# HGRN2's values and K turned by VectorE and small transfers instead of TensorE, from the third unit on

## The chip, the core and the metric

The kernel runs on one core of a Trainium2 chip. A core has TensorE (PE, matrix products; the loading of its stationary operand is listed as PEld), VectorE (DVE), ScalarE (ACT), GpSimd (POOL) and SyncE (SP), whose queue issues nearly all transfers. Transfers run on 16 DMA engines. Everything lies in HBM at first; work is done on tiles of 128 partitions in SBUF, and TensorE writes to PSUM. The metric is the device time of one execution in microseconds, as the median of several runs. Before the change it is 2566.66 us (three runs, 2566.41 to 2567.90).

## The reference, cut to what matters

One decoder layer in float32, for 16 meta tokens and 256 prompt tokens, and for 8 further sequences with one new token each and a stored state. D_MODEL is 2048, D_FF 5504.

```python
x = layer_norm(ALPHA * x + 0.5 * swiglu(x, f1_g, f1_u, f1_d), ln1_g, ln1_b)
m, s_ret, s_hg = token_mixer(x, pos, s_ret, s_hg, prompt, w_in, lb, hg_norm_g, w_out)
x = layer_norm(ALPHA * x + m, ln2_g, ln2_b)
x = layer_norm(ALPHA * x + 0.5 * swiglu(x, f2_g, f2_u, f2_d), ln3_g, ln3_b)
```

The mixer projects x to ten parts of 2048 columns. Retention (8 heads of 256) uses q_r, k_r, v_r, g_r; HGRN2 (16 heads of 128) uses q_h, f_h, i_h, g_h; a_r and a_h gate the two branches. HGRN2 of one chunk is:

```python
f = lb + (1.0 - lb) * jax.nn.sigmoid(f_h)        # k = 1 - f, values v = i_h
o = jnp.einsum('bhij,bhjv->bhiv', A, v) + jnp.einsum('bhid,bhdv->bhiv', q * jnp.exp(b), S)
S_new = jnp.exp(b_last)[..., None] * S + jnp.einsum('bhjd,bhjv->bhdv', k_dec, v)
```

Outputs are the two groups of tokens and the new states of both branches for both groups.

## The kernel before

All 280 tokens (16 meta, 256 prompt, 8 sampled) stand as columns; features stand on partitions. A weight block is 128x128. Products keep float32 precision by splitting both operands into an upper and a lower part: three matmuls a block (`xh,whi`, `xl,whi`, `xh,wlo`, line L218). Weights come in units of 8 blocks, 512 KB each: SP loads `raw` (L185), ScalarE casts it to `whi` (L188), VectorE takes the difference `wlo` (L189). `raw`, `whi` and `wlo` have three buffers each, so a load waits until VectorE has used up the unit three before, and a cast until TensorE has.

The stages are: first FFN (up, down), mixer with its input projection (`pj_...`), output projection (`wo`), second FFN. The mixer goes over eight units u, each one head of retention and two of HGRN2. For a unit, `project` runs ten groups of two output tiles: f, q_h, i_h, q_r, k_r, v_r of unit u, and then four groups of gates (g_r with a_r, g_h with a_h, twice) of unit u-1's outputs. A group is 16 dense steps, one for each block of the inner dimension, with six matmuls a step; a group ends in `evacuate`.

TensorE's order is the order in which the program is written. After each dense step `pump` counts every thread down by one and lets those at zero issue their next piece. HGRN2's thread (`mix_hg`) is started when i_h is evacuated, retention's (`mix_ret`) when v_r is. A `yield n` in a thread is a pause of n dense steps. So the numbers behind `yield` and in `start` say between which dense matmuls a piece of the mixer stands. The order on the other engines and on SP's queue is set by a scheduler from data dependences and priorities; weight loads have high priority. Eight completion semaphores go round over SP's transfers, so a transfer waits for the one eight places before it.

In HGRN2's thread the steps that matter here are: the values v (features on partitions) are transposed to `vt` with tokens on partitions (tile `vth`; L875, copied out at L879), together with the short `ends` of meta and sampled tokens (L878); after the levels of decay products, `turned(h)` transposes K of each head (L982, copied to `kth` at L983); `load` and `values` fetch the sampled states (`smh`) and broadcast values (`vbh`), each behind a one-column copy on GpSimd (L769, L773) that makes them wait; `samples` updates the sampled states; `pst` (L1022, L1024) multiplies K and v to the states, which VectorE scales and adds (`Sh`, L1027) and SP stores (`out_sgp`, L1030); `pq` (L1039) and `po` (L1050, L1051) make the outputs. Retention's thread transposes its own v and k (L1107, L1114), makes `psr` (L1168), loads two megabytes of sampled states (`smr`, L1095), scales them on ScalarE (L1192), adds to them on VectorE (L1198) and stores them (`out_srs`, L1202), then makes `pqr` (L1211) and `por` (L1226).

## Time and profile before

| what | before |
|---|---|
| median of the runs | 2566.66 us |
| span of the profiled execution | 2563.9 us |
| instructions | 56275 |
| PE busy | 2553.4 us |
| DVE busy | 1702.8 us |
| ACT busy | 1392.2 us |
| bytes moved | 536.26 MB, 209 GB/s in the mean |
| granted TensorE clock | 1.000 |

The table's span is that of one profiled execution; the page gives no other time for it, and the runs' median is 2.8 us above its span. A view by lines groups instructions by line, engine and tiles: a line such as `L875 PE MATMUL pt<-ident,v` reads "line 875, TensorE, writes pt from ident and v". Durations of matmuls in it overlap, since matmuls are pipelined: the time from one start to the next is what TensorE's order costs. In a view of waits a line is "engine and tile <- what it waited for: us in total, times, longest". In a timeline a row is start, duration, engine, line, operation, tiles, shape, count, and in brackets the idle time before it. A unit of the mixer from the third on takes the same 126.3 us each (the first f of the fourth unit starts at 1085.64, of the fifth at 1211.98).

### The profile page before, as it was taken

Reading aid. Unit: us, or ns where it says so; the run is one execution under the profiler, and the core shown is the slowest. Engines: PE = TensorE matmul, PEld = TensorE weight load, DVE = VectorE, ACT = ScalarE, POOL = GpSimd, SP = SyncE. Lnnn points to the kernel's source line nnn. Section 1 sums busy time; section 2 is a strip of 40 time slices with the busy share of each in tenths; the row PEclk is TensorE's granted clock in tenths of the full one; section 3 lists DMA queues with packets and bytes.
Section 4 is the critical chain, followed back from the end, with each engine's and each line's share of the span. In section 5 each row is a group of like instructions: output and inputs, shape, how many; then the busy total and the mean of one; then the engine's idle time right before and its main releaser. Section 6 shows DMA issues by size and latency. Waiting matters only on the chain.

```text
span 2563.9 us, 56275 instructions
## 1 busy us (share of the span) xinstructions
PE 2553.4 (100%) x23424; PEld 2534.4 (99%) x23424; DVE 1702.8 (66%) x2827; ACT 1392.2 (54%) x2186; POOL 57.0 (2%) x152
## 2 busy tenths in 40 slices
PE   9999999999999999999999999999999999999999
PEld 9999999999999999999999999999999999999998
DVE  6444544475569878777777777777885555556555
ACT  5444444444456767767676666675564444444443
POOL 0000000000000000000000000000000000000000
PEclk9999999999999999999999999999999999999999
DMA  7555555555555876767676767675556565565554
GB/s 244 183 187 183 187 182 184 186 182 186 184 201 180 287 265 232 264 214 260 212 264 215 259 223 255 224 239 188 196 190 197 194 197 195 194 196 195 195 195 149
DMA packets 156897, 536.26 MB, mean 209 GB/s; under 512 B 17952, under 2 KB 25952, under 8 KB 156640
## 3 DMA queue, kind: packets, MB, share of 16 engines
q1 hardware_dynamic: 156352, 532.37, 62.0%
q8 instruction: 183, 3.00, 0.5%
q14 instruction: 74, 0.61, 0.1%
q10 hardware_dynamic: 288, 0.29, 0.0%
HBM read 501.99 MB, written 30.61 MB: 208 GB/s over the span
## 4 chain that ended last, share of the span: by engine, by line
PE 96%; DVE 2%; ACT 0%; issue 0%; DMA 0%; SPq 0%; ACTq 0%; DVEq 0%
PE up L218 36%; PE dn L218 19%; PE pj_i_h L218 3%; PE pj_g_r L218 3%; PE pj_q_h L218 3%; PE pj_g_h L218 3%; PE pj_a_r L218 3%; PE pj_a_h L218 3%; PE pj_f L218 3%; PE pj_q_r L218 3%; PE pj_k_r L218 3%; PE wo L218 3%; PE pj_v_r L218 3%; DVE wlo L189 1%; PE pqr L1211 1%; PE psr L1168 0%
## 5 line engine op out<-in xcount | busy, mean ns | idle before, releaser
L189 DVE TENSOR_TENSOR wlo<-raw,whi 128x1024 fp32r<-128x1024 f32 (+1 forms) x869 | 1062.2, 1223 | 740.7 <-ACT whi L188 737.3
L188 ACT CAST whi<-raw 128x1024 fp32r<-128x1024 f32 (+1 forms) x870 | 905.7, 1042 | 909.2 <-PE up L218 411.0
L218 PE MATMUL up<-xh,whi 128*128 128x280 f32 (+1 forms) x2624 | 725.6, 280 | 0.6 <-ACT whi L188 0.6
L218 PE MATMUL up<-xh,wlo 128*128 128x280 f32 (+1 forms) x2624 | 725.8, 280 | 0.4 <-DVE wlo L189 0.3
L218 PE MATMUL up<-xl,whi 128*128 128x280 f32 (+1 forms) x2624 | 725.4, 279 | 0.0
L218 PEld LDWEIGHTS up<-xh,wlo 128*128 128x128 f32 x2624 | 492.6, 189 | 1.0 <-DVE wlo L189 1.0
L218 PEld LDWEIGHTS up<-xh,whi 128*128 128x128 f32 x2624 | 492.6, 189 | 0.8 <-ACT whi L188 0.8
L218 PEld LDWEIGHTS up<-xl,whi 128*128 128x128 f32 x2624 | 492.6, 189 | 0.0
L218 PE MATMUL dn<-hh,whi 128*128 128x280 f32 (+1 forms) x1376 | 384.7, 280 | 0.0
L218 PE MATMUL dn<-hh,wlo 128*128 128x280 f32 (+1 forms) x1376 | 384.3, 279 | 0.0
L218 PE MATMUL dn<-hl,whi 128*128 128x280 f32 (+1 forms) x1376 | 384.3, 279 | 0.0
L218 PEld LDWEIGHTS dn<-hh,whi 128*128 128x128 f32 x1376 | 260.1, 189 | 0.1
L218 PEld LDWEIGHTS dn<-hl,whi 128*128 128x128 f32 x1376 | 260.1, 189 | 0.1
L218 PEld LDWEIGHTS dn<-hh,wlo 128*128 128x128 f32 x1376 | 260.1, 189 | 0.0
L218 PE MATMUL pj_k_r<-xh,whi 128*128 128x280 f32 x256 | 74.2, 290 | 0.0
L218 PE MATMUL pj_g_r<-xh,whi 128*128 128x264 f32 x256 | 74.0, 289 | 0.0
L218 PE MATMUL pj_v_r<-xh,whi 128*128 128x280 f32 x256 | 73.8, 288 | 0.0
L218 PE MATMUL pj_v_r<-xh,wlo 128*128 128x280 f32 x256 | 72.4, 283 | 0.3 <-DVE wlo L189 0.3
L218 PE MATMUL pj_g_h<-xh,whi 128*128 128x264 f32 x256 | 72.7, 284 | 0.0
L218 PE MATMUL pj_k_r<-xh,wlo 128*128 128x280 f32 x256 | 72.4, 283 | 0.0
L218 PE MATMUL pj_v_r<-xl,whi 128*128 128x280 f32 x256 | 72.3, 283 | 0.0
L218 PE MATMUL pj_k_r<-xl,whi 128*128 128x280 f32 x256 | 72.3, 283 | 0.0
(421 smaller groups left out, 5263.4 us busy)
## 6 DMA issues: line engine op xcount, KB each, us to landing
raw<-in_w_up SPq DMA_DIRECT2D x343, 512.0 KB, 4.1
raw<-in_w_in SPq DMA_DIRECT2D x320, 512.0 KB, 4.3
raw<-in_w_dn SPq DMA_DIRECT2D x172, 512.0 KB, 3.5
smr<-in_sr SPq DMA_DIRECT2D x32, 512.0 KB, 5.0
out_srs<-smr SPq DMA_DIRECT2D x32, 512.0 KB, 6.7
raw<-in_w_out SPq DMA_DIRECT2D x32, 512.0 KB, 3.9
vbr<-vrd SPq DMA_DIRECT2D x32, 256.0 KB, 4.1
smh<-in_sg SPq DMA_DIRECT2D x16, 512.0 KB, 5.2
```

Source lines behind the costliest of these rows:

```text
L188: nc.scalar.copy(hi[:, j:jn, :], raw[:, j:jn, :])
L189: nc.vector.tensor_tensor(out=lo[:, j0:j1, :], in0=raw[:, j0:j1, :], in1=hi[:, j0:j1, :].bitcast(F32), op=ALU.subtract)
L218: nc.tensor.matmul(o, w, t, start=start, stop=stop)
L1211: nc.tensor.matmul(pq[32 * j : 32 * j + 32, :256], qdr_at[c][:, 32 * b : 32 * b + 32], sms[2 * e + c][:, j, :], start=e + c == 0, stop=e + ...
```

## The change

From the third unit on (u > 1, or c0 > 2), v and K are no longer transposed by TensorE. VectorE turns 32x32 blocks within a tile, and 16 transfers of 32 partitions x 4 x 32 elements put the blocks in their places, one after two dense steps each, issued by a small thread of their own (`turned_over`).

- For v, VectorE reads the projection's PSUM directly (two instructions of 128x256) into the tile `v`, the transfers go to `vt`, and ScalarE copies the 16 first and 16 last columns of each head to `ends`. The two copies of v by ScalarE, the two by GpSimd, four transposes and two copies out of PSUM fall away.
- For K, VectorE turns both heads in one instruction (128x512) into the tile of k, which is dead by then, and the transfers go to the tile of f, also dead. Four transposes and two copies out of PSUM fall away. The waits of `load(1)` and `values(1)` now look at these tiles.
- The pause ahead of `pst` becomes 30 for 5, the one behind it 20 for 45.
- Retention's thread is started with 5 for 3 in these units, and a later pause in it is 13 for 15.

```diff
                 elif n == "i_h":
-                    v = st.pop("i_h", None)
-                    if v is None:
+                    v, vt = st.pop("i_h", None), tmp("vth", TURNED)
+                    ends = tmp("ends", (P, 2, 2, NMETA))
+                    if c0 > 2:
+                        z = squared(tmp("v", (P, 2, T)))
+                        for j, o in enumerate((o0, o1)):
+                            nc.vector.transpose(z[:, j].rearrange("p b t -> p (b t)"), o[:, NMETA:LP])
+                            nc.scalar.copy(ends[:, j, 0, :], o[:, :NMETA])
+                            nc.scalar.copy(ends[:, j, 1, :], o[:, T - NMETA : T])
+                        turned_over(vt, z, 2)
+                    elif v is None:
                         v = tmp("v", (P, 2, T))
                         nc.scalar.copy(v[:, 0, :], o0)
                         nc.scalar.copy(v[:, 1, :], o1)
-
-                    start(mix_hg(c0 // 2, st["f"], st["k"], st["q"], v), {0: 20, 2: 46}.get(c0, 4))
+                    start(mix_hg(c0 // 2, st["f"], st["k"], st["q"], v, ends, vt), {0: 20, 2: 46}.get(c0, 4))
...
-                    start(mix_ret(c0 // 2, st["q_r"], st["k_r"], v), 24 if c0 == 2 else 3)
+                    start(mix_ret(c0 // 2, st["q_r"], st["k_r"], v), {0: 3, 2: 24}.get(c0, 5))
...
+            TURNED = (P, 2, 2, P)
+            squared = lambda x: x.rearrange("p h t -> p (h t)")[:, : 4 * P].rearrange("p (h b t) -> p h b t", h=2, b=2)
...
+            def turned_over(out, z, pause):
+
+                def transfers():
+                    for i in range(0, P, 32):
+                        for j in range(0, P, 32):
+                            nc.sync.dma_start(out[j : j + 32, :, :, i : i + 32], z[i : i + 32, :, :, j : j + 32])
+                            yield pause
+
+                start(transfers(), 1)
...
-            def mix_hg(u, f, k, q, v):
+            def mix_hg(u, f, k, q, v, ends, vt):
...
-                ends = tmp("ends", (P, 2, 2, NMETA))
-                nc.gpsimd.tensor_copy(ends[:, :, 0, :], v[:, :, :NMETA])
-                nc.gpsimd.tensor_copy(ends[:, :, 1, :], v[:, :, T - NMETA :])
+                if u < 2:
+                    nc.gpsimd.tensor_copy(ends[:, :, 0, :], v[:, :, :NMETA])
+                    nc.gpsimd.tensor_copy(ends[:, :, 1, :], v[:, :, T - NMETA :])
...
-                    nc.gpsimd.tensor_copy(sms[h][:, 0, :1], kts[0][:, 0, :1] if h else acc[:, 15:16])
+                    nc.gpsimd.tensor_copy(sms[h][:, 0, :1], (kts[0] if u < 2 else k)[:, 0, :1] if h else acc[:, 15:16])
...
-                    nc.gpsimd.tensor_copy(vbs[h][:, 0, :1], kts[1][:, 0, :1] if h else acc[:, 2 * P + 15 : 2 * P + 16])
+                    n = 32 if h and u > 1 else P
+                    nc.gpsimd.tensor_copy(vbs[h][:n, 0, :1], kts[1][:n, 0, :1] if h else acc[:, 2 * P + 15 : 2 * P + 16])
...
-                    pt = mx_bank("pt")
-                    for b in range(2):
-                        nc.tensor.transpose(pt[:, b * P : (b + 1) * P], v[:, h, NMETA + b * P : NMETA + (b + 1) * P], ident)
+                    if u < 2 or h:
+                        pt = mx_bank("pt")
+                    if u < 2:
+                        for b in range(2):
+                            nc.tensor.transpose(pt[:, b * P : (b + 1) * P], v[:, h, NMETA + b * P : NMETA + (b + 1) * P], ident)
...
-                kts = []
+                kts = [squared(f)[:, h] for h in range(2)] if u > 1 else []
 
                 def turned(h):
+                    if u > 1:
+                        if h == 0:
+                            z = squared(k)
+                            nc.vector.transpose(z.rearrange("p h b t -> p h (b t)"), K[:, :, NMETA:])
+                            turned_over(squared(f), z, 2)
+                        return
...
-                    yield 4 if u == 0 else 5
+                    yield 4 if u == 0 else 30
...
-                yield (8, 11, 45)[min(u, 2)]
+                yield (8, 11, 20)[min(u, 2)]
...
-                yield (11 if u == 0 else 15) + 2 * calm
+                yield (11, 15, 13)[min(u, 2)] + 2 * calm
```

How this moves instructions shows in three places, all in the fourth unit (u=3). The first is TensorE around K's first pair of transposes (`ptk`) before the change, between two dense steps of k_r (the numbers behind the names are those of buffers):

```order
L218 MATMUL pj_k_r_14433<-xl_9_9272,whi_14546 128x280
L218 MATMUL pj_k_r_14433<-xh_9_9271,wlo_14547 128x280
L982 MATMUL ptk<-ident,K 128x128 x2
L218 MATMUL pj_k_r_14432<-xh_10_9275,whi_14546 128x280
L218 MATMUL pj_k_r_14432<-xl_10_9276,whi_14546 128x280
```

In the changed kernel k_r's dense steps follow each other there, while `pst`, which stood in v_r, now stands within the first g_h group, between its seventh and eighth step:

```order
L218 MATMUL pj_a_h_15043<-xh_6_9259,wlo_15121 128x264
L1050 MATMUL pst<-vm,km 128x128
L1052 MATMUL pst<-vth,f 128x128 x2
L1050 MATMUL pst<-vm,km 128x128
L1052 MATMUL pst<-vth,f 128x128 x2
L218 MATMUL pj_g_h_15042<-xh_7_9263,whi_15120 128x264
```

The second place is SP's queue between k_r and the start of retention's transfers, in the changed kernel (`f<-k` are K's small transfers):

```order
L185 DMA raw_15044<-in_w_in 128x1024
L1030 DMA out_sgs<-smh 128x1024
L185 DMA raw_15119<-in_w_in 128x1024
L741 DMA f<-k 32x4x32 x2
L185 DMA raw_15167<-in_w_in 128x1024
L741 DMA f<-k 32x4x32 x5
L185 DMA raw_15209<-in_w_in 128x1024
L741 DMA f<-k 32x4x32
L749 DMA vrd<-vt_8636 8x256
L185 DMA raw_15251<-in_w_in 128x1024
L1184 DMA vbr<-vrd 128x512 x2
```

Before, only weight loads, `out_sgs` and `out_sgp` stood there; the small transfers of v stand likewise, in runs of 4, 3, 3 and 6, between the weight loads during q_r, and `out_sgp` now follows the second `out_srs`.

The third place is VectorE in the g_h group and behind it, where retention's sampled states (`smr`) are updated between the weights' differences (`wlo`). Before:

```order
L189 TENSOR_TENSOR wlo_15175<-raw_15173,whi_15174 128x8x128
L189 TENSOR_TENSOR wlo_15217<-raw_15215,whi_15216 128x8x128
L1198 SCALAR_TENSOR_TENSOR smr<-vbr,sro,smr 128x256 x5
L189 TENSOR_TENSOR wlo_15247<-raw_15245,whi_15246 128x8x128
L1198 SCALAR_TENSOR_TENSOR smr<-vbr,sro,smr 128x256 x3
L240 TENSOR_TENSOR gt<-gs,pj_g_h_15035 128x264
L189 TENSOR_TENSOR wlo_15277<-raw_15275,whi_15276 128x8x128
```

And in the changed kernel, the same four units of weights (`wlo_15211`, `wlo_15253`, `wlo_15283`, `wlo_15313`):

```order
L189 TENSOR_TENSOR wlo_15211<-raw_15209,whi_15210 128x8x128
L1226 SCALAR_TENSOR_TENSOR smr<-vbr,k_r,smr 128x256 x2
L1055 SCALAR_TENSOR_TENSOR Sh<-Sh,T_14522,pst 128x128 x4
L189 TENSOR_TENSOR wlo_15253<-raw_15251,whi_15252 128x8x128
L1226 SCALAR_TENSOR_TENSOR smr<-vbr,sro,smr 128x256 x2
L189 TENSOR_TENSOR wlo_15283<-raw_15281,whi_15282 128x8x128
L1226 SCALAR_TENSOR_TENSOR smr<-vbr,sro,smr 128x256 x5
L189 TENSOR_TENSOR wlo_15313<-raw_15311,whi_15312 128x8x128
```

`Sh` has come in ahead of the second of these, and the five updates that stood ahead of the third now stand ahead of the fourth.

6 lines of the change are left out of this document (3 added, 3 removed).

## The prediction

> **What bounds the kernel now.** I read the page first: the span, the busy times and the chain of waits.
>
> ```profile
> span 2563.9 us, 56275 instructions
> PE 2553.4 (100%) x23424; PEld 2534.4 (99%) x23424; DVE 1702.8 (66%) x2827; ACT 1392.2 (54%) x2186; POOL 57.0 (2%) x152
> PE 96%; DVE 2%; ACT 0%; issue 0%; DMA 0%; SPq 0%; ACTq 0%; DVEq 0%
> ```
>
> TensorE is busy all the time and is 96% of the chain. So the time is the sum of what TensorE issues, as long as nothing makes it wait. Next I cut one steady unit of the mixer, the fourth (u=3), into three stretches with the view of busy time by window; the columns are the stretch, its length, busy time and instructions of PE, PEld, DVE, ACT and POOL, the granted clock, the DMA share and GB/s.
>
> ```profile
> 1085.64:1168.00 82.36, 82.36 (x848) 81.84 (x847) 66.39 (x135) 56.60 (x111) 4.75 (x11) 1.00 0.64 216
> 1168.00:1194.00 26.00, 26.00 (x275) 24.96 (x274) 21.21 (x39) 15.90 (x24) 1.40 (x3) 1.00 0.84 281
> 1194.00:1211.98 17.98, 17.98 (x159) 17.88 (x158) 10.87 (x22) 12.30 (x25) 0.00 (x0) 1.00 0.77 275
> ```
>
> A unit takes 126.34 us, at full clock, with no gap on TensorE. But the slack beneath differs. ScalarE's casts of the weights (`whi`) tell it, by what they wait for. These are ScalarE's waits in two stretches of the same unit, 1120 to 1165 and then 1168 to 1194:
>
> ```profile
> ACT whi L188 <- PE pj_q_r L218: 4.6, 2, 2.9
> ...
> ACT whi L188 <- DMA raw<-in_w_in: 5.7, 3, 2.3
> ```
>
> In the first the cast waits for TensorE to give a buffer back, so the weights are early. In the second it waits for the transfer itself. How close that comes to TensorE, two rows of the timeline show: the last step of one 512 KB of weights (`wlo`, VectorE), and the first matmul that reads it (matched by counting the weights' units back from the end of the program).
>
> ```profile
> 1184.59 1.22 DVE L189 TENSOR_TENSOR wlo<-raw,whi 128x1024 fp32r<-128x1024 f32 x1
> 1186.05 0.28 PE L218 MATMUL pj_g_r<-xh,wlo 128*128 128x264 f32 x1
> ```
>
> The weights are ready at 1185.81 and needed at 1186.05: 0.24 us ahead. I call this the dip. It lies where retention loads and stores its sampled states, and recurs in every unit.
>
> **The change, part by part.** *Removed on TensorE.* Four pairs of transposes a unit, two of v (one of them with the `ends` transpose, which stays) and two of K. Their price on TensorE's path is not their recorded duration but by how much the matmuls behind them start later:
>
> ```profile
> 1121.97 0.28 PE L218 MATMUL pj_q_r<-xh,wlo 128*128 128x264 f32 x1
> 1122.09 0.38 PE L875 MATMUL pt<-ident,v 128*128 128x128 f32 x2
> 1122.22 0.36 PE L218 MATMUL pj_q_r<-xh,whi 128*128 128x264 f32 x1
> 1122.42 0.28 PE L218 MATMUL pj_q_r<-xl,whi 128*128 128x264 f32 x1
> 1122.53 0.28 PE L218 MATMUL pj_q_r<-xh,wlo 128*128 128x264 f32 x1
> ...
> 1140.10 0.28 PE L218 MATMUL pj_k_r<-xh,wlo 128*128 128x280 f32 x1
> 1140.22 0.38 PE L982 MATMUL ptk<-ident,K 128*128 128x128 f32 x2
> ...
> 1140.56 0.28 PE L218 MATMUL pj_k_r<-xl,whi 128*128 128x280 f32 x1
> 1140.68 0.28 PE L218 MATMUL pj_k_r<-xh,wlo 128*128 128x280 f32 x1
> ```
>
> Dense matmuls start 0.11 us apart (1122.42, 1122.53; 0.12 with 280 columns: 1140.56, 1140.68). From 1121.97 to the second matmul behind the first pair, at 1122.42, is 0.45; two steps would be 0.225, so the pair costs 0.22. K's pair: 1140.10 to 1140.56, 0.46 less 0.24, again 0.22. Each transpose thus costs what a dense matmul does, with no further price for breaking in, so I take the pair that leaves `ends` behind at 0.22 too. A unit saves 4 x 0.22 = 0.88 us, and the counts say that a unit has four of each transpose:
>
> ```profile
> L982 PE MATMUL ptk<-ident,K 128*128 128x128 f32 x32 | 6.1, 273 | 0.0
> L875 PE MATMUL pt<-ident,v 128*128 128x128 f32 x32 | 6.1, 273 | 0.0
> ```
>
> Of the eight units six change: 6 x 0.88 = **5.3 us**.
>
> *Added on VectorE.* Two turnings of 128x256 from PSUM and one of 128x512. The trace has none; the nearest rows are:
>
> ```profile
> 1135.24 0.43 DVE L677 SCALAR_TENSOR_TENSOR q_r<-pj_q_r,cos 128x264 f32<-128x264 f32 x1
> 1111.40 0.69 DVE L240 TENSOR_TENSOR Q<-q,f 128x512 f32<-128x512 f32 x1
> ```
>
> I take 2 x 0.43 + 0.69 = 1.55 us a unit, and twice that, 3.1, as the upper end; nothing can be under 0. They stand in the first stretch, where the weights wait for TensorE, and where VectorE is idle for 16 of 82 us: 0 on the path. Without that cover a unit would pay the 1.55 to 3.1. ScalarE loses two copies of v and four out of PSUM and gains four narrow ones: it gets lighter.
>
> *Added on SP and the DMA engines.* 32 transfers a unit, 16 KB each in 128-byte runs. One load of the kernel's start has exactly this size and number of packets (`lbt`), and one microsecond there held almost only small packets:
>
> ```profile
> lbt<-in_lb SPq DMA_DIRECT2D x1, 16.0 KB, 4.2
> 27.44 0.42 SPq L539 DMA_DIRECT2D lbt<-in_lb  x1
> ...
> DMA packets 228, 0.11 MB, mean 106 GB/s; under 512 B 212, under 2 KB 212, under 8 KB 227
> q1 hardware_dynamic: 227, 0.09, 32.7%
> q1 hardware_dynamic: 156352, 532.37, 62.0%
> ```
>
> SP is held 0.42 us by each. The longest run of them between two weight loads is six, 2.5 us, while the loads are a weight unit apart: 24 matmuls of 0.11 to 0.12, 2.7 to 2.9 us. So they fit, just. On the engines, 32.7% of 16 engines in that microsecond is 5.2 us for 227 packets, 23 ns each at most: 128 x 23 / 16 = 0.18 us a transfer, 5.9 us a unit. The upper end is the run's mean packet, nearly all of 4 KB: 62% x 16 x 2563.9 / 156352 = 163 ns, 1.3 us a transfer, 42 us a unit. The first stretch has 36% of 82 us free, 30 us. The first price disappears in it, the second does not (a rival). I take the first, from the row of the same size. The Trainium skill (DMA: Bandwidth & Descriptors, Specifications) says that writes under 512 B are read, modified and written; by that the price would lean to the upper end, but the small packets of this trace show no sign of it.
>
> *Moved.* HGRN2's state products (`pst`) leave `v_r` for the first `g_h` group, 25 steps later, and take their followers along: VectorE's `Sh`, ScalarE's copy, SP's two `out_sgp`. That is now inside the stretch of the dip. Retention starts two steps (12 matmuls, 1.35 us) later there, but its last part is where it was (13 for 15).
>
> ```profile
> 1154.95 0.28 PE L218 MATMUL pj_v_r<-xh,wlo 128*128 128x280 f32 x1
> ...
> 1156.31 0.28 PE L218 MATMUL pj_v_r<-xl,whi 128*128 128x280 f32 x1
> ...
> 1156.77 0.43 ACT L1025 COPY Sh<-pst 128x128 f32<-128x128 f32 x2
> 1157.93 1.12 DVE L1027 SCALAR_TENSOR_TENSOR Sh<-Sh,T,pst 128x128 f32<-128x128 f32 x4
> 1184.20 0.48 DVE L1198 SCALAR_TENSOR_TENSOR smr<-vbr,sro,smr 128x256 f32<-128x256 f32 x1
> ```
>
> `pst` costs TensorE 1.36 less 0.24, 1.12 us, in either place. In its new place it delays TensorE's need for the dip's weights by that 1.12, while VectorE gets 1.12 and ScalarE 0.43 more to do. Behind `Sh` on VectorE stands a `wlo`, and TensorE waits for that. On the other side, the dip's own `wlo` has two state updates ahead of it where it had five: 3 x 0.48 = 1.4 us less. I therefore put the dip at 0.24 + 1.12 + 1.4 - 1.12 - 0.43 = 1.2 us, no stall; the bounds are 2.7 us (ScalarE and VectorE hide theirs) and a stall (below). K's last transfer is issued some 45 steps less 31 before `pst`, 14 steps or 9 us, so 4.2 us of landing fit.
>
> **Sum.** 2563.9 - 5.3 = 2558.6 us of span. The median of the runs, 2566.66, is 2.8 above the profiled span; so 2566.66 - 5.3 = **2561.4 us**, 0.21% less. What a measurement tells from no change is 0.2%, 5.1 us, and the forecast lies almost on that line.
>
> **Rivals.** *The dip becomes a stall* (slower). Retention's work comes 1.35 later, `Sh` and the copy add 1.55, and only 0.24 of slack and the 1.12 of `pst` stand against it: 1.35 + 1.55 - 1.36 = 1.5 us a unit, 9.2 in all, 2570.6; if the 1.12 does not help, 2.7 a unit, 16, 2577. It outweighs the gain from 0.88 us a unit, and shows as slower from 0.88 + 0.86 = 1.7. For it: the weights there already wait for the DMA, at 84% share. Against it: the order of VectorE's rows, above. *A small stall*, 0.1 to 0.8 us a unit, takes the gain back: 2562 to 2566, no measurable difference. *The transfers cost like other packets* (slower): 42 us in 30 leaves 12 us late a unit, of which the two weight units in stock bridge at most 5.4; 6.6 x 6 - 5.3 gives about 2601. It decides from 30 us a unit, 117 ns a packet, five times the row's 23. *A transpose costs its recorded 273 ns*: 48 x 0.273 = 13.1 us, 2553.6. Against it stands the start of the next matmul, 0.13 us after that of the two. The Trainium skill (VectorE: DVE Perf Modes, The three transpose paths) gives 390 ns for a 128x128 on TensorE; by this the saving would be an estimated 18.7 us, which the trace's 0.11 contradicts. By the same page's Rules for kernel authors a 128x128 belongs on TensorE if PSUM will do as its destination: that speaks against this change, and at 0.11 each there is indeed little to win.
>
> **How the numbers follow.** The forecast has 0.68 (0.44 of it beyond 0.2%, 0.24 short of it, since the line is inside its own spread of some 0.7 us); the small stall 0.17; the stall that makes it slower 0.09; dear packets 0.03; dear transposes 0.03. Faster: 0.44 + 0.03 = 0.47. The same: 0.24 + 0.17 = 0.41. Slower: 0.09 + 0.03 = 0.12. The range runs from 2560.2 (a little more, where the dip in some runs already cost something) to 2566.5 (all of the gain lost to small stalls), and leaves out the three dear cases and the outermost of the forecast.
>
> **What would show it.** Right: TensorE's matmuls fewer by 48, a steady unit of 125.45 us instead of 126.34, PE still busy throughout 1168 to 1194, and the dip's `wlo` more than 1 us ahead of its matmul. Wrong: gaps of PE in front of a matmul that reads `wlo` or `whi` late in the `g_h` group or early in the second `g_r` group; ScalarE's casts waiting for DMA between `q_r` and `v_r`; a turning on VectorE over 1.4 us; or `pst` waiting for `f` or `vth`. The forecast fails if the six units are not each about 0.9 us shorter.

## The result, and the profile after

The changed kernel takes 2578.68 us (2577.52 to 2584.51) where the kernel before took 2566.6 us on the same chip. The ratio is 1.0052 with a 95% interval of 1.0037 to 1.0066: **slower by 0.5%**, where 2561.4 us had been forecast. The span of the profiled execution grew by 11.8 us. The 5.3 us that the removed transposes were to save must be added, so about 17 us of new stall have to be explained.

The page of the changed kernel, its span, its engines and its chain of waits:

```profile
span 2575.7 us, 56433 instructions
PE 2555.1 (99%) x23376; PEld 2532.6 (98%) x23376; DVE 1708.0 (66%) x2845; ACT 1382.1 (54%) x2174; POOL 45.9 (2%) x140
PE 87%; DVE 5%; DMA 4%; ACT 2%; issue 1%; SPq 0%; POOL 0%; ACTq 0%; DVEq 0%
```

TensorE has 48 matmuls fewer, as meant. But its share of the chain fell from 96% to 87%: VectorE, DMA and ScalarE, 2% together before, now hold 11% of the chain. The same unit as in the prediction (u=3) starts its f here, and the next unit here:

```profile
1089.42 0.28 PE L218 MATMUL pj_f<-xh,whi 128*128 128x280 f32 x1
...
1217.04 0.28 PE L218 MATMUL pj_f<-xh,whi 128*128 128x280 f32 x1
```

That is 127.62 us a unit, not the 125.45 expected; the next three take 127.75, 127.14 and 127.25. So each of these four has a stall of about 2 us. The third unit takes 136.46 where it took 133.39, and from the last unit's start to the first matmul of the output projection it is 172.67 us where it was 169.83: about 4 us of stall in each of these two, with the 0.88 saved. That is 15.6 of the 17 us; the rest lies outside, ahead of the third unit and in the output projection and behind it.

The busy times in the three stretches of this unit, at the same distances from its start as in the prediction (the last one is longer by what the unit grew):

```profile
1089.42:1171.78 82.36, 82.36 (x847) 81.84 (x846) 67.35 (x136) 56.40 (x110) 3.77 (x9) 1.00 0.70 218
1171.78:1197.78 26.00, 24.37 (x252) 23.52 (x254) 20.96 (x40) 14.51 (x22) 0.42 (x3) 1.00 0.83 276
1197.78:1217.04 19.26, 19.26 (x180) 18.58 (x172) 11.33 (x24) 12.12 (x24) 0.00 (x0) 1.00 0.86 291
```

The first stretch, which holds all the turning and all the small transfers, has no gap. TensorE stands in the second, the dip (24.37 of 26.00 us busy), although that stretch moves no more bytes than before (0.83 and 276 GB/s against 0.84 and 281). Rows of SP, VectorE and TensorE show in order how it comes about (times from the span's start; in brackets the idle time before):

```profile
1165.78 4.26 SPq L741 DMA_DIRECT2D f<-k  x5
...
1170.71 0.59 SPq L741 DMA_DIRECT2D f<-k  x1
1171.35 0.49 SPq L749 DMA_DIRECT2D vrd<-vt  x1
...
1173.92 0.85 SPq L1184 DMA_DIRECT2D vbr<-vrd  x2
...
1178.09 0.48 DVE L1226 SCALAR_TENSOR_TENSOR smr<-vbr,k_r,smr 128x256 f32<-128x256 f32 x1 [1.81 <-DMA vbr<-vrd]
...
1188.69 0.88 DVE L1226 SCALAR_TENSOR_TENSOR smr<-vbr,sro,smr 128x256 f32<-128x256 f32 x2 [2.64 <-DMA vbr<-vrd]
1189.48 1.22 DVE L189 TENSOR_TENSOR wlo<-raw,whi 128x1024 fp32r<-128x1024 f32 x1
1190.76 0.38 PE L218 MATMUL pj_g_r<-xh,wlo 128*128 128x264 f32 x1 [1.48 <-DVE wlo L189]
```

`vrd` and `vbr` bring retention's sampled values to all partitions. SP issues them behind K's last small transfers, and VectorE stands in front of its state updates until `vbr` has landed: 1.81 us for the first pair, 2.64 for the second. Behind the second wait in VectorE's order stands a `wlo`, and TensorE waits 1.48 us for it. In the kernel before, `vrd` and `vbr` were issued here:

```profile
1162.40 0.29 SPq L730 DMA_DIRECT2D vrd<-vt  x1
...
1164.42 0.80 SPq L1156 DMA_DIRECT2D vbr<-vrd  x2
```

Counted from the start of the unit that is 76.9 and 78.9 us before, 81.9 and 84.5 after: 5.0 and 5.6 us later, though retention's thread was moved by two steps, 1.35 us. (The unit before starts at 1085.48 by the row of its first f, not at 1085.64 as given above; its length is the same.) Moreover `v_r`, behind which retention starts, now ends 70.0 us into the unit instead of 72.0. By its place in the program `vrd` was thus due a little earlier than before, not later (one_straight, below, issues it at 75.6).

The chain of waits in the changed kernel says how one late wait is passed on (VectorE, then a weight load that can only start when VectorE gives its buffer back, then both halves of the split, then VectorE's own order):

```profile
1179.76 1.67 DVE smr L1226 x4
1181.43 1.15 DVE wlo L189
1182.59 5.39 DMA raw<-in_w_in
1188.08 1.04 ACT whi L188
1189.48 1.22 DVE wlo L189
1190.70 1.98 DVE smr L1226 x5
1192.68 1.15 DVE wlo L189
1193.87 0.38 PE pj_g_r L218
```

So the 1.48 us come mainly down this chain, from the first wait on `vbr`: the cast `whi` ended at 1189.12, and the second wait held the `wlo` back only from there to 1189.48.

One more loss follows in the profiled execution. Behind its longest wait for a `wlo` (1.86 us, in the last unit) the profile grants half the clock for 3.41 us; the columns are those of the busy times above:

```profile
1698.76:1702.19 3.43, 1.57 (x14) 1.38 (x13) 3.37 (x7) 1.59 (x3) 0.00 (x0) 1.00 0.76 307
1702.19:1705.60 3.41, 3.41 (x18) 3.41 (x18) 3.27 (x7) 0.35 (x2) 0.00 (x0) 0.50 0.90 279
```

Dense matmuls start 0.22 us apart there instead of 0.11, which is 1.7 us lost. The kernel before has no such stretch ahead of its last few microseconds.

The view of waits over all steady units (950 to 1800 us) gives this for the kernel before (two lines), and then for the changed one (three lines); the numbers are us in total, times, longest:

```profile
ACT smr L1192 <- DMA smr<-in_sr: 4.8, 8, 1.3
DVE smr L1198 <- DMA vbr<-vrd: 0.2, 1, 0.2
```

```profile
ACT smr L1220 <- DMA smr<-in_sr: 22.7, 12, 3.7
DVE smr L1226 <- DMA vbr<-vrd: 19.7, 10, 3.3
PE pj_g_r L218 <- DVE wlo L189: 7.6, 7, 1.9
```

So retention's data come late in two places: `vbr` on VectorE, and the sampled states `smr` themselves on ScalarE, where a cast `whi` stands behind. I call both **late data**.

### The profile page after: what moved, and what is told of

Its sections match the earlier page's. It is cut to its first block, busy times and chain, and to the rows that moved or that the text cites. A ratio compares the mean times of both kernels' runs of the same rounds, so it can differ in the third digit from the quotient of the medians.

```text
span 2575.7 us, 56433 instructions
## 1 busy us (share of the span) xinstructions
PE 2555.1 (99%) x23376; PEld 2532.6 (98%) x23376; DVE 1708.0 (66%) x2845; ACT 1382.1 (54%) x2174; POOL 45.9 (2%) x140
## 4 chain that ended last, share of the span: by engine, by line
PE 87%; DVE 5%; DMA 4%; ACT 2%; issue 1%; SPq 0%; POOL 0%; ACTq 0%; DVEq 0%
PE up L218 35%; PE dn L218 19%; PE pj_q_h L218 3%; PE pj_f L218 3%; PE wo L218 3%; PE pj_i_h L218 3%; PE pj_q_r L218 3%; PE pj_k_r L218 2%; PE pj_g_h L218 2%; PE pj_a_h L218 2%; PE pj_g_r L218 2%; PE pj_a_r L218 2%; DVE wlo L189 2%; PE pj_v_r L218 2%; DMA raw<-in_w_in 1%
## 5 line engine op out<-in xcount | busy, mean ns | idle before, releaser
L218 PE MATMUL pj_g_r<-xh,wlo 128*128 128x264 f32 x256 | 72.7, 284 | 8.4 <-DVE wlo L189 7.6
```

The source lines that it names most:

```text
L218: nc.tensor.matmul(o, w, t, start=start, stop=stop)
```

## The experiments

The table gathers the runs on which the argument rests. "Saved" is what TensorE saves by the transposes left out, at 0.44 us a unit for v and 0.44 for K. "Stall" is the median time against that of the kernel before on the same chip, plus what was saved. The two columns behind it are the two waits just shown, in us over the steady units. They are read from one profiled execution, whose time can lie some us beside the median that the stall is taken from; the last column says how far. So the waits tell where a kernel stands still, and compare only roughly in size.

| kernel | transfers for each turning | retention starts | saved | time - before | stall | VectorE on vbr | ScalarE on smr | profiled - median |
|---|---|---|---|---|---|---|---|---|
| before | - | 3 | 0 | 0 | 0 | 0.2 | 4.8 | |
| v_only | 16 | 3 | 2.6 | -1.8 | 0.9 | 3.9 | 3.0 | +1.6 |
| four_v | 5 | 3 | 2.6 | -2.4 | 0.3 | 5.3 | 1.8 | +1.5 |
| only_pst | - | 3 | 0 | +0.7 | 0.7 | 3.1 | 1.4 | -0.8 |
| only_ret | - | 5 | 0 | +10.2 | 10.2 | 5.9 | 17.8 | 0.0 |
| moves_only | - | 5 | 0 | +6.5 | 6.5 | 11.2 | 18.6 | -0.9 |
| k_only | 16 (K) | 5 | 2.6 | +4.8 | 7.5 | 16.9 | 20.7 | -3.0 |
| the change | 16 | 5 | 5.3 | +12.1 | 17.4 | 19.7 | 22.7 | -1.2 |
| ret_one | 16 | 4 | 5.3 | +15.7 | 21.0 | 7.8 | 26.0 | +1.1 |
| ret_back | 16 | 3 | 5.3 | +5.7 | 11.0 | 5.1 | 16.2 | -0.1 |
| free_ret | 16 | 3 | 5.3 | +7.0 | 12.3 | 6.9 | 17.2 | -1.5 |
| vbr4 | 16 | 5 | 5.3 | +9.4 | 14.7 | 11.7 | 31.1 | +1.4 |
| pool_scale | 16 | 5 | 5.3 | +11.8 | 17.1 | 20.7 | - | +3.9 |
| one_straight | 1 | 5 | 5.3 | +4.5 | 9.8 | 12.5 | 18.2 | +0.6 |
| four_reads | 5 | 5 | 5.3 | +1.2 | 6.5 | 15.1 | 14.7 | +4.2 |
| straight_ret | 1 | 3 | 5.3 | -0.2 | 5.1 | 3.9 | 4.2 | +3.3 |
| four_ret3 | 5 | 3 | 4.4 | +3.0 | 7.4 | 4.8 | 14.9 | +3.5 |

### One part at a time: v_only, k_only, moves_only

v_only takes only the values' part of the change, k_only only K's with the moves, moves_only only the pauses and starts, all from the kernel before:

```diff
# moves_only, against the kernel before
-                    yield 4 if u == 0 else 5
+                    yield 4 if u == 0 else 30
-                yield (8, 11, 45)[min(u, 2)]
+                yield (8, 11, 20)[min(u, 2)]
-        start(mix_ret(...), 24 if c0 == 2 else 3)
+        start(mix_ret(...), {0: 3, 2: 24}.get(c0, 5))
-                yield (11 if u == 0 else 15) + 2 * calm
+                yield (11, 15, 13)[min(u, 2)] + 2 * calm
```

> Only the values v are turned by VectorE and placed by small transfers; K goes back to TensorE, and pst and retention stand where they stood before. Three theories for the 17 us that the change lost beside the 5.3 us it saved. SP: its queue is held by K's transfers (0.60 us each in the trace of the change, with waits for earlier ones), and what stands behind them is late for retention; v's transfers stand where the weights are 3 to 5 us ahead, so only the saving of 24 transposes shows, 2.6 us: 2564.0. DMA engines: the small packets slow all transfers; half of them, half the loss: 2566.6 - 2.6 + 8.5 = 2572.5. Moves: pst and retention's later start do the harm; without them 2564.0.

> Only K is turned by VectorE and placed by small transfers, with pst and retention moved as in the change; v goes back to TensorE. SP: the whole loss stays, 2566.6 - 2.6 + 17 = 2581. DMA engines: half of it, 2572.5. Moves: the whole loss, 2581.

> Nothing is turned by VectorE, all transposes are on TensorE as before; only pst stands 25 steps later and retention starts two steps later, as in the change. SP: TensorE has the same work and the queue is free, so 2566.6, at most 2 us more. DMA engines: 2566.6. Moves: the whole loss without the saving, 2584.

Measured: v_only 2565.50 us (ratio 0.9995, 0.9985 to 1.0005), k_only 2572.07 (1.0021, 1.0012 to 1.0031), moves_only 2573.78 (1.0026, 1.0015 to 1.0037). The moves alone, without any turning, lose 6.5 us. In v_only three of the four steady units take 125.9 us, which is 126.34 less the 0.44 of v's two pairs (the fourth takes 127.3): the price of the transposes holds, and sixteen small transfers a unit, without the moves, do no harm that the medians can tell. k_only has less stall than the whole change by 10 us, so the parts don't add up.

### Which move: only_ret, only_pst

Each has one of the two moves alone, on the kernel before: retention's (the last two pairs of lines above) or `pst`'s (the first two).

> The kernel before with retention's shift alone (5 and 13 for 3 and 15); pst stays in v_r, no turning. It splits the 6.5 us that the moves cost together. Theory 'broadcast': retention's broadcast is issued two steps later and lands later, VectorE waits for it (about 11 us in all, as with both moves; 1.8 before), and the time is 2571 to 2574. Theory 'followers': the cost is pst's followers, which stay where they were, and the time is 2566.5 to 2568.

> The kernel before with pst's move alone (pauses 30 and 20 for 5 and 45), retention as before, no turning. Theory 'broadcast': vbr is issued and lands as before, VectorE's waits on it stay under 4 us, and the time is 2566.5 to 2568.5. Theory 'followers': the four Sh in front of a wlo and the two stores in the dip cost about 1 us a unit, 2571 to 2574.

Measured: only_ret 2577.16 us (1.0035, 1.0023 to 1.0046), only_pst 2567.71 (1.0001, 0.9991 to 1.0011). This is the clearest pair of the study. Moving `pst`, with its four `Sh` on VectorE and its two stores, into the dip costs nothing that can be measured; a steady unit is again 126.33 us. Starting retention two dense steps later costs 10 us by itself. Here are its waits, and its chain of waits through the dip of a later unit:

```profile
ACT smr L1192 <- DMA smr<-in_sr: 17.8, 11, 3.5
...
PE pj_g_r L218 <- DVE wlo L189: 7.0, 7, 1.7
```

```profile
1431.46 7.49 DMA smr<-in_sr
1439.12 0.99 issue
1440.11 1.04 ACT whi L188
1441.17 1.24 DVE wlo L189
1442.42 4.68 DMA raw<-in_w_in
1447.49 1.05 ACT whi L188
1448.54 1.23 DVE wlo L189
1449.82 0.38 PE pj_g_r L218
```

`smr` takes 7.49 us to land, and ScalarE stands before it with a cast of weights behind. In the kernel before, ScalarE hardly waits for the same load (fourth unit: SP's issue, then ScalarE's use):

```profile
1171.73 0.41 SPq L1095 DMA_DIRECT2D smr<-in_sr  x1
1176.55 1.15 ACT L1192 ACTIVATE smr<-smr,sro 128x1024 f32<-128x1024 f32 x1 [0.50 <-DMA smr<-in_sr]
```

From the fourth unit on the kernel before issues this load 86.3 us into the unit, and ScalarE uses it 4.4 to 4.8 us later; only_ret issues it at 87.6 to 87.8, and ScalarE can use it only 6.0 to 7.6 us later. So ScalarE has the data not 1.35 us later, but 2.7 to 4.3. Two loads of `smr` go out here, and in only_ret a weight load leaves SP between them (at 88.5 to 88.7), while in the kernel before the next one leaves at 91.2, behind both. That the three then share the DMA engines is the obvious reading; no run varies this alone. The late data, then, do not need the small transfers at all. With `pst` in the dip as well (moves_only) the loss is 3.6 us smaller by the medians, though the two intervals overlap. It would fit that TensorE needs its weights 1.12 us later there, as the prediction had reckoned.

### Retention's start put back: ret_back, ret_one, free_ret

```diff
# ret_back, against the change (ret_one: 4 and 14)
-        start(mix_ret(...), {0: 3, 2: 24}.get(c0, 5))
+        start(mix_ret(...), 24 if c0 == 2 else 3)
-                yield (11, 15, 13)[min(u, 2)] + 2 * calm
+                yield (11 if u == 0 else 15) + 2 * calm
# free_ret: in addition
-    nc.gpsimd.tensor_copy(vbs[h][:n, 0, :1], kts[1][:n, 0, :1] if h else ...)
+    nc.gpsimd.tensor_copy(vbs[h][:n, 0, :1], (kts[1][:n] if u < 2 else k[:n, 1:, :])[:, 0, :1] if h else ...)
```

> The changed kernel with retention's start and its later pause as before (3 and 15 for 5 and 13); turning, small transfers and pst's new place stay. Theory 'broadcast': SP issues vrd behind K's last small transfers (81.9 us after the unit's start, 76.9 before the change), and that doesn't move with retention's start, so vbr stays late; at most the 1.35 us of the two steps come back in units where vrd could go between the transfers: 2572 to 2579. Theory 'retention's start': the two steps are the cause, and the time falls by most of the 17 us of stall, to 2562 to 2566. Theory 'followers': no change, 2577 to 2580.

> The changed kernel with retention started one dense step later than before the change instead of two (4 and 14 for 5 and 13). With two it is 2578.7, with none 2572.7, where the first transposes of retention wait for ScalarE's copies of v and GpSimd's tails instead. Theory 'late data': between the two there is a place where both waits are small: 2566 to 2571, with TensorE's wait for tails under 1 us in all and the second g_r group's stall about half of 2 us a unit. Theory 'SP': retention's start matters little beside the transfers: 2573 to 2578.

> The changed kernel with retention's start as before (3 and 15), and with GpSimd's one-column copy ahead of the second load of vbh looking at HGRN2's turned k, not at the tile that K's small transfers write. So vbh no longer waits until K's first transfer has landed, and neither GpSimd nor SP stands there (4.7 us a unit on SP in the changed kernel). With retention's start alone put back it was 2572.7. Theory 'late data': SP and GpSimd are free earlier, the sampled states smh come earlier, and ScalarE's copies of v are no longer late: part or all of the 0 to 2 us a unit in the first g_r group goes, 2563 to 2570. Theory 'ScalarE': v is late because v_r is 2 us shorter than before while ScalarE's work ahead of v is the same; then nothing changes, 2571 to 2575.

Measured: ret_back 2572.70 us (1.0023, 1.0014 to 1.0033), ret_one 2582.25 (1.0056, 1.0041 to 1.0071), free_ret 2573.52 (1.0025, 1.0015 to 1.0035). Retention as before wins back 6.4 us. Of what is left, a part lies in another place, at retention's first transposes (waits of ret_back):

```profile
PE pt L1144 <- POOL tails L1131: 4.4, 5, 1.0
...
PE pt L1135 <- ACT v L691: 2.1, 3, 1.0
```

`v_r` now ends about 2 us earlier (0.88 of transposes and 1.12 of `pst` are gone in front of its end), while ScalarE has the same sampled HGRN2 states to scale ahead of its copies of v. So retention's first transposes wait for the copies: a start two steps later avoids this wait and gets the other. One of the two theories for free_ret, that GpSimd's wait for K's first transfer was behind it, was wrong: freeing it changed nothing that could be measured. And the middle start, ret_one, is not between the two: it is worse than ret_back, and by the medians also worse than the change, though there the intervals overlap. Its rows show two things. SP issues the two loads of `smr` 0.4 to 0.7 us apart, where 2.5 us lie between them in the kernel before, and ScalarE then waits 3.8 to 4.6 us for the first in each of the last five units. And its profiled execution has two stretches of 3.41 us at half the clock, each beginning in a wait of TensorE or within 1.1 us behind one, which lose 3.4 us in all; the changed kernel has one such stretch. Why the two loads go out together was not settled.

### The gates: vbr4, pool_scale

vbr4 gives the second pair of `vbr` tiles of its own (dead ones), so that all four are loaded at once; pool_scale lets GpSimd, instead of ScalarE, scale the second half of `smr`.

```diff
# vbr4, against the change
-                spread(0)
-                spread(1)
+                for i in range(2 if u < 2 else 4):
+                    spread(i)
# pool_scale, against the change
-                        nc.scalar.activation(sm, sm, AF.Copy, scale=gams[e])
+                        if e and u > 1:
+                            nc.gpsimd.tensor_scalar(out=sm, in0=sm, scalar1=gams[e], scalar2=None, op0=ALU.mult)
+                        else:
+                            nc.scalar.activation(sm, sm, AF.Copy, scale=gams[e])
```

> The changed kernel with one edit: from the third unit on, the second two of retention's four broadcast tiles (vbr) get places of their own (the tiles of v and of HGRN2's k, both dead by then), so all four are loaded together, before VectorE has used up the first two. The state updates, the small transfers and the moves stay. Theory 'broadcast': in the changed kernel VectorE stands before retention's state updates until vbr has landed (21.9 us in all, 2.6 us in the fourth unit's second half), the weights' differences wlo stand behind it, and SP can issue the second pair of vbr only behind a weight load that itself waits for VectorE. With own places the second half's wait goes: VectorE's waits on vbr fall from 21.9 to about 11 (the first halves stay), most of the 2.1 us a unit in the second g_r group goes, and the time is 2563 to 2569. Theory 'engines full': the weights are late because the DMA engines carry more in that stretch (84 to 85% share); then loading vbr earlier changes nothing, 2576 to 2580. Theory 'followers': VectorE has too much to do there with the four Sh behind pst; also 2576 to 2580.

> The changed kernel with the second half of retention's sampled states (smr) scaled by GpSimd instead of ScalarE from the third unit on; all else as in the change. ScalarE then no longer stands before smr until it has landed (22.7 us of waits in the change) with a cast whi behind it; VectorE still stands before vbr and smr. Theory 'ScalarE's wait': the casts come earlier, a good part of the stall of about 2 us a unit goes, 2566 to 2573. Theory 'VectorE's wait': the wlo behind VectorE's state updates are what TensorE waits for, and these come no earlier, later if GpSimd's scaling is slow: 2577 to 2585.

Measured: vbr4 2576.37 us (1.0034, 1.0021 to 1.0047), pool_scale 2578.86 (1.0045, 1.0031 to 1.0059). The first theory, that most of the stall would go with vbr4, failed. The waits of vbr4, then of pool_scale:

```profile
ACT smr L1224 <- DMA smr<-in_sr: 31.1, 11, 5.1
DVE smr L1230 <- DMA vbr<-vrd: 11.7, 6, 2.6
```

```profile
DVE smr L1229 <- DMA vbr<-vrd: 20.7, 12, 2.8
PE pj_g_r L218 <- DVE wlo L189: 8.7, 12, 1.1
```

Earlier `vbr` shortens VectorE's wait on it from 19.7 to 11.7 us, and ScalarE's on `smr`, now behind more transfers, grows from 22.7 to 31.1. Taking ScalarE out of the way leaves VectorE where it was. But neither edit takes away just one wait: in pool_scale GpSimd needs 3.4 us for a tile that ScalarE scales in 1.15, so the data are also ready later. The rows suggest two gates one behind the other, where opening one moves the wait to the other. That either wait alone is the cause is not borne out; that both together are it was not shown by an edit either, only by the rows.

### The transfers: one_straight, sixteen_straight, four_reads, straight_ret

```diff
# one_straight (straight_ret: the same, with retention's start put back)
-                    for i in range(0, P, 32):
-                        for j in range(0, P, 32):
-                            nc.sync.dma_start(out[j : j + 32, :, :, i : i + 32], z[i : i + 32, :, :, j : j + 32])
-                            yield pause
+                    nc.sync.dma_start(out, z)
+                    yield pause
# four_reads
+                    scr = drp.tile([P, 2, 2, P], F32, tag="turn", name="turn")
+                    nc.sync.dma_start(scr, z)
+                    yield 12
+                    for j in range(0, P, 32):
+                        nc.sync.dma_start(
+                            out[j : j + 32].rearrange("p h b (i t) -> p (h b) i t", i=4),
+                            scr[:, :, :, j : j + 32].rearrange("(i p) h b t -> p (h b) i t", i=4))
+                        yield pause
# sixteen_straight
+                    for i in range(0, P, 8):
+                        nc.sync.dma_start(out[i : i + 8], z[i : i + 8])
+                        yield pause
```

> The changed kernel with one straight transfer (128 partitions, 2 KB each) in place of each sixteen small ones; the placing of the blocks is left out, so the HGRN2 values and K that the products read are in the wrong places. Turning on VectorE, pst's place and retention's two steps stay. It takes away SP's 16 x 0.6 us twice a unit and nearly all small packets. Theory 'late data': the stall comes from retention starting two steps later, since ScalarE and VectorE then stand before sampled states (smr, vbr) that land later; that alone cost 10 us in the kernel before, so the time stays at 2571 to 2577, and ScalarE's waits for smr stay near 18 us. Theory 'SP': the small transfers hold back weight loads, vrd and vbr, and without them the gain comes out: 2561 to 2564.

> The changed kernel with sixteen transfers as before, one after two dense steps, but each straight: 8 partitions of 2 KB in place of 32 partitions x 4 x 32 elements. The placing of the blocks is left out, so HGRN2's values and K stand in the wrong places. Number of instructions on SP as in the change (32 a unit), packets 128 instead of 2048 for each sixteen. With one straight transfer the time was 2571.1, with sixteen small ones 2578.7: 7.6 us between them. Theory 'instructions': SP's queue is what the small transfers cost, by their number: 2575 to 2580, vrd and vbr as late as in the change. Theory 'packets': SP is held 0.60 us by each because of its many short runs; with 0.35 us each and few packets the time is that of one transfer, 2569 to 2573.

> One straight transfer in place of each sixteen (the placing is left out, values and K stand in the wrong places), and retention's start as before the change (3 and 15). So it has what the change saves on TensorE and pst's new place, but neither the small transfers nor the two steps. Theory 'late data': what is left of the stall with one transfer (2571.1, 9.9 us above the full gain) is that of retention's two steps, which alone cost 10 us in the kernel before; without them the gain comes out, 2561 to 2564. Theory 'ScalarE': with the transposes and pst gone from the stretch in front, v_r ends 2 us earlier against ScalarE's work, retention's first transposes wait for ScalarE's copy of v and GpSimd's tails whatever the transfers do: 2568 to 2573, with TensorE's wait for v and tails 4 us or more.

> The changed kernel with the blocks placed in another way: the turned tile is written to HBM in one transfer, and 12 dense steps later four transfers of 32 partitions read it back to its places. Five instructions on SP instead of sixteen, the same short runs on the reading side. The result is complete. Theory 'instructions': it comes near the time with one straight transfer, 2570 to 2574. Theory 'packets': the short runs cost the same on the engines and SP is held longer by each of the four: 2576 to 2581.

one_straight, straight_ret and sixteen_straight leave the placing of the blocks out, so values and K stand in the wrong places; they serve for the time alone.

Measured: one_straight 2571.06 us (1.0016, 1.0006 to 1.0025), four_reads 2568.28 (1.0004, 0.9994 to 1.0013), straight_ret 2566.85 (0.9999, 0.9990 to 1.0009), sixteen_straight 2609.18 (1.0163, 1.0148 to 1.0178). four_reads does all the work of the change, with as many 128-byte packets (24704 in either execution), and is 10.8 us faster than it, each taken against the kernel before on its chip, by 5 instructions on SP in place of 16. So it is not the packets but the sixteen transfers on SP's queue that cost, 8 to 11 of the 17.4 us. Whether it is the 9.6 us that they hold SP (2.7 in four_reads), or that they are spread over 32 dense steps (20 in four_reads), was not separated. In four_reads SP issues `vrd` 76.3 us after the unit's start (1088.99), and `vbr` at 80.5, against 81.9 and 84.5:

```profile
1164.63 0.60 SPq L743 DMA_DIRECT2D f<-turn  x1
1165.32 0.58 SPq L753 DMA_DIRECT2D vrd<-vt  x1
...
1169.53 0.80 SPq L1188 DMA_DIRECT2D vbr<-vrd  x2
```

Taking away the two steps as well (straight_ret) brings the stall from 9.8 to 5.1 us, and ScalarE's and VectorE's late data to 4.2 and 3.9 us, near those of v_only. In its profiled execution, 3.3 us above the median, 3.7 us are again waits of TensorE for tails and v at retention's start, and 2.0 for `wlo`. sixteen_straight does not tell what it was meant to: the scheduler spread these transfers further, K's last ones were issued 92 to 93 us into the unit from the fourth on (80 to 82 in the change), and TensorE stood at `pst` itself, with the clock at half for 6.83 us around this wait:

```profile
1190.48 1.20 PE L1051 MATMUL pst<-vth,f 128*128 128x128 f32 x4 [4.33 <-DMA vrd<-vt]
```

### Other ways: pool_queue, pst_near, four_v, four_ret3

pool_queue issues the small transfers from GpSimd's queue. pst_near has retention as before, `pst` six steps later instead of 25 and one K transfer a step. four_v turns only the values, with four_reads' five transfers, and moves nothing. four_ret3 is four_reads with retention as before, from the fourth unit on.

```diff
# pool_queue
-                            nc.sync.dma_start(out[j : j + 32, ...], z[i : i + 32, ...])
+                            nc.gpsimd.dma_start(out[j : j + 32, ...], z[i : i + 32, ...])
# pst_near, beside ret_back's lines
-                            turned_over(squared(f), z, 2)
+                            turned_over(squared(f), z, 1)
-                    yield 4 if u == 0 else 30
+                    yield 4 if u == 0 else 11
-                yield (8, 11, 20)[min(u, 2)]
+                yield (8, 11, 39)[min(u, 2)]
```

> The change with one edit: the small transfers are issued by GpSimd, which is busy for 2% of the span, and no longer by SP. Same transfers, same packets, same moves. SP: the loss goes, 2561.3, at most 2564 if GpSimd's issue makes the transfers land later. DMA engines: the loss stays, 2578.7. Moves: the loss stays, 2578.7.

> The changed kernel with retention's start as before (3 and 15), pst only six dense steps later than before the change (still in v_r, pauses 11 and 39), and K's small transfers one a step instead of one every second step, so that they have landed by then. So v_r keeps its 1.1 us of pst. Theory 'ScalarE': retention's v is then copied in time, TensorE's waits on v and tails go, and since retention starts as before there is no late data either: 2562 to 2566. Theory 'SP': sixteen transfers of 0.6 us in 16 steps of 0.7 us hold SP throughout, weight loads come late during k_r and v_r, or pst waits for K: over 2570.

> Only the values turned by VectorE from the third unit on, and placed by way of HBM (one transfer out, four back) instead of sixteen small transfers; K on TensorE, pst and retention as in the kernel before. Five instructions on SP a unit. TensorE saves 6 x 0.44 = 2.6 us. Theory 'late data' and theory 'instructions' agree here: nothing is moved later, SP's queue is hardly longer, so the gain comes out, 2563.5 to 2565 beside 2567.0 before (2565.5 with sixteen). Against both: a steady unit above 126.0 us.

> Values and K turned by VectorE and placed by way of HBM (five transfers in place of sixteen) from the fourth unit on instead of the third, pst 25 steps later in these units, retention's start as before the change (3 and 15) in all. TensorE saves 5 x 0.88 = 4.4 us. With one straight transfer and retention's start as before the stall was 5.4 us, 4.1 of it in the third unit's k-to-g_r stretch and the last units. Theory 'late data': with SP nearly free and retention not moved, the stall is 1 to 3 us: 2563.5 to 2566. Theory 'ScalarE' (retention's first transposes wait for v and tails because v_r is shorter): 0.5 to 1.5 us a unit, 2565 to 2570.

Measured: pool_queue 2598.81 us (1.0120, 1.0105 to 1.0136), pst_near 2643.55 (1.0295, 1.0280 to 1.0311), four_v 2565.11 (0.9992, 0.9983 to 1.0001), four_ret3 2570.49 (1.0012, 1.0003 to 1.0021). GpSimd is held 0.55 us by each transfer; its queue also has the tails, the gates' copies and `gam`, and TensorE then waits for ScalarE's casts too, which it doesn't in the change's steady units (waits of pool_queue):

```profile
PE pj_g_r L218 <- ACT whi L188: 10.1, 6, 2.8
```

So emptying SP's queue by filling another one is no cure here; how the 32 us divide was not settled. pst_near shows that six steps are too few for `pst`: even with K's transfers one a step it waits for them in each of the six units, and the granted clock is at half for 10 to 14 us around each of these waits (0.985 in the mean of the execution, 0.999 in the change's).

```profile
PE pst L1052 <- DMA f<-k: 64.0, 6, 11.3
```

four_v is the fastest kernel of the study, 2.4 us under the kernel before, but its interval just reaches 1: no difference that was measured for certain. four_ret3 was expected at 2563.5 to 2566 by late data and at 2565 to 2570 by ScalarE's copies; it lies above both, with stalls up to 4 us in single units. No version that turns K too beat the kernel before.

## Why the prediction was wrong

**Removed on TensorE: right.** 5.3 us at 0.11 us a transpose. The steady unit of v_only shows 0.44 of 0.88 directly.

**Added on VectorE: right.** 1.55 us a unit had been taken from neighbouring rows. The rows of the tiles give 2 x 0.424 + 0.700 = 1.55, and the stretch around them has no gap:

```profile
L669 DVE STREAM_TRANSPOSE v<-pj_i_h x12: 403/424/444, 995.9 to 1633.5; 128x256 f32<-128x256 f32 x12
L1002 DVE STREAM_TRANSPOSE k<-K x6: 699/700/701, 1015.0 to 1652.4; 128x512 f32<-128x512 f32 x6
```

**Added on SP: the first step that failed.** "SP is held 0.42 us by each ... so they fit, just." The row of `lbt` had the same bytes and number of packets but another form, and the small transfers take half as long again:

```profile
L741 SPq DMA_DIRECT2D f<-k x96: 585/599/1681, 1017.9 to 1678.7; - x96
```

Six at 0.60 are 3.6 us, more than the 2.7 to 2.9 between two weight loads, and a run of five was seen to take 4.26, waits included. The prediction weighed them only against the weight loads around them, which are early there. It did not ask what else stands behind them in SP's queue: `vrd` and `vbr`, 5.0 and 5.6 us later in the fourth unit. By one_straight and four_reads the sixteen transfers cost 8 to 11 us of the stall, with the two steps in place, where 0 had been put.

**Added on the DMA engines: right.** 5.9 us a unit had been estimated; the first stretch's DMA share rose from 0.64 to 0.70 of 82.36 us, 4.9 us.

**Moved, `pst` and its followers: right.** No cost in its new place (only_pst), and K's last transfer was issued 8.5 us ahead of it (1170.71 and 1179.22) where 9 had been worked out.

**Moved, the dip: the second step that failed.** "I therefore put the dip at 1.2 us, no stall"; it became a wait of 1.48 us in the unit shown. The sum counted what VectorE and ScalarE have to do and took from the order of their rows that fewer updates stand in front of the `wlo`. But these updates don't start when VectorE is free; they start when `vbr` and `smr` have landed. Retention's two steps stand at 1.35 us in the rival's sum and not at all in that of the dip; alone they cost 10.2 us, 1.7 a unit (only_ret), and in its rows ScalarE has `smr` 2.7 to 4.3 us later, not 1.35.

**The rivals.** "The dip becomes a stall", with a chance of 0.09 and 2570.6 to 2577, is what happened, in the place named and a little beyond the time named. Its working was half right: retention's delay counts, the `Sh` and the copy don't. The argument that kept it at 0.09, the order of VectorE's rows, says nothing on when their data land. That the total came so near the rival's 2577 is partly luck, since its sum has neither SP's queue nor the half clock in it. Dear packets and dear transposes did not occur. The Trainium skill (VectorE: DVE Perf Modes, Rules for kernel authors) had spoken for TensorE for a 128x128 transpose if PSUM will do as its destination. This case agrees in the outcome, though not through VectorE's own price, which was hidden: what was dear is the placing of the 32x32 blocks behind it.

**What stays open.** The stall is not a sum of parts: retention's two steps cost 10.2 us in the kernel before, 4.7 with one transfer and 6.4 with sixteen. Why the two loads of `smr` meet when retention starts one step later, what lengthens their landing, and whether the 5.1 us left in straight_ret could be won by other places for ScalarE's copies of v, the runs don't tell.

## What to carry to other kernels

Where an in-order engine does both the work that the bottleneck needs next and updates on data from a transfer, a delay of that transfer can be a delay of the bottleneck, however much idle time the engine shows. So for every transfer that a change adds or moves, list what stands behind it in the issuing queue, and follow those transfers to the engine that waits for them and to what stands behind there. A shift need not stay what it is: here 1.35 us in the program became 2.7 to 4.3 us for the data. And count transfers, not bytes: placing blocks by five transfers instead of sixteen of the same short runs was worth some ten microseconds here, twice what the whole change was to save.

## What was not expected of the hardware

How long SP is held by a transfer hangs on its form, not on its bytes or runs alone: 0.42 us for `lbt` (16 KB), 0.60 for 32 partitions of 4 x 32 elements, 0.64 for 8 partitions of 2 KB, 0.57 for 32 partitions read back from HBM (64 KB), 0.48 for 128 partitions of 2 KB (256 KB). On the DMA engines a 128-byte packet took 13 ns, so the 128 of one small transfer are 0.10 us of sixteen engines, a sixth of what they cost SP. The Trainium skill (DMA: Bandwidth & Descriptors, Issuing engines are not separate DMA queues) calls the issuing time usually small beside the transfer itself. Here it is six times the DMA engines' own 0.10 us, so the sentence does not hold of that, and the measurement decides. Beside the time to landing the issue is small here too: in pool_queue, where the profile has it, 0.55 us beside medians of 3.4 and 5.0.

A wait of TensorE of 1.86 us was enough for the profile to show half the clock for 3.41 us behind it. In four_ret3 two waits of 0.8 us close together were followed by such a stretch, while a single wait of 1.48 us in the change was not. What decides it these traces don't show.
